# Two output projections: four Strassen units instead of three, with weight sums made by accumulating DMAs

## The chip, the core and the metric

The kernel runs on one core of a Trainium2 chip. A core has five engines that run independent instruction streams and meet only at semaphores: TensorE (PE in the profile; PEld is its weight load), VectorE (DVE), ScalarE (ACT), GpSimd (POOL) and SyncE (SP). Tensors sit in HBM, tiles in SBUF, and matmul results in banks of PSUM. DMAs move data between HBM and SBUF; SP issues most of them, GpSimd some, each from its own queue in the order of its program. The metric is the device time of one execution in microseconds (us).

## The reference, cut to what matters

Two layers on 512 tokens of width 1024, all in float32: an attention mixer, then an mLSTM mixer, each followed by a gated feed-forward block. The change touches only the second matrix of that block, `w_out`:

```python
D_FF = 2816
def swiglu(xn, w_in, w_out):
    gu = xn @ w_in
    return (jax.nn.silu(gu[..., :D_FF]) * gu[..., D_FF:]) @ w_out
...
h = h + swiglu(rms_norm(h, ffn_norm[i]), ffn_w_in[i], ffn_w_out[i])
```

So each layer multiplies a hidden matrix of 512 tokens by 2816 with weights of 2816 by 1024 and adds the result to the residual stream. After layer 1 a last norm follows.

## The kernel before

*Precision.* A float32 operand is split into a high part (rounded by a ScalarE copy, `split_chunk` L204 to L211 for weights, `split_operand` L1110 to L1116 for the hidden values) and a low part (VectorE: operand minus high part). Each product is made of three matmuls: high by high, high by low, low by high.

*Row tiles.* The 2816 rows of `w_out` are 22 tiles of 128, taken in pairs: 11 pairs `pi`. The hidden matrix is kept as `hid[pi]`, two row tiles by 512 tokens; `half(pi, t)` is one of its two halves of 256 tokens. The 1024 output columns form two halves n of 512.

*Units.* `output_products` (L1090) joins pair u with pair UNITS + u for u = 0, 1, 2. A unit is a 2 x 2 block product (two pairs by two column halves of weights, two pairs by two token halves of hidden values), and is computed as seven block products P1 to P7 (the Strassen-Winograd scheme) instead of eight. It needs sums of weight blocks and sums of hidden halves. The pairs left over, 6 to 10 (`REST`), are multiplied in the plain way, one item for each pair and column half.

*A product's weights.* `prepare_product` (L1121) loads the blocks that the product needs (512 KB each, SP's queue, tag `wraw` with three buffers; the block W11 goes to `tw`, tag `w8`, and stays there to become the running sum T; the second block of P5 in layer 0 goes to tag `t1`, one buffer). VectorE forms the sum, then `split_chunk` makes the high and low part (three buffers each), and the hidden operand is split. So the split of item n waits until TensorE has finished item n - 3. Layer 0 and layer 1 use two mirrored variants (`sums_of_rows` true and false): in layer 0 the matmuls of a product have 256 columns (tokens) and there are 24 of them, in layer 1 they have 512 columns (weights) and there are 12.

*Order.* `items` (L1211) lists the work: P1 of all units, P5 and P2 in turn, P6 and P7 with the first column half of the plain pairs between them, P3, then P4 with the second column half between, and a few plain items as a tail. `work` prepares an item two items (AHEAD) before its matmuls are issued; the first two are prepared while the input projection `ffn_in` still runs. `during` (L1189) runs in `ffn_in`'s blocks j and forms sums of hidden halves there, and in the last block it splits the operands of P1 and P2. The order of instructions on each engine is that of a scheduler which follows program order closely but moves ready work forward; within an engine the order is then fixed. After some products `then` (L1284, L1673) copies or adds banks of PSUM.

Of the kernel before, what the change touches and what calls it, by code (L numbers as in the profile page):

```python
# [11 lines left out]
F32 = mybir.dt.float32  # L12
F32R = mybir.dt.float32r
I32 = mybir.dt.int32
AF = mybir.ActivationFunctionType
ALU = mybir.AluOpType
# [55 lines left out]
def tile_hybrid_dilated_attn_mlstm(  # L72
# [124 lines left out]
    def load_chunk(src, shape, name):  # L197
        n = int(np.prod(shape[1:]))
        view = lambda t: t[:, :n].rearrange("p (a b) -> p a b", a=shape[1])
        raw = wp.tile([P, 1024], F32, tag="wraw", name=name + "_w", bufs=W_BUFS)  # L200
        nc.sync.dma_start(view(raw), src)
        return raw, n, view, name

    def split_chunk(chunk):  # L204

        raw, n, view, name = chunk
        hi = wp.tile([P, 1024], F32R, tag="whi", name=name + "_h", bufs=W_BUFS)
        lo = wp.tile([P, 1024], F32R, tag="wlo", name=name + "_l", bufs=W_BUFS)
        nc.scalar.activation(hi[:, :n], raw[:, :n], AF.Copy)
        nc.vector.tensor_tensor(lo[:, :n], raw[:, :n], hi[:, :n].bitcast(F32), op=ALU.subtract)  # L210
        return view(hi), view(lo)  # L211
# [878 lines left out]
    def output_products(layer, fp, wo, sums_of_rows, tail):  # L1090
# [3 lines left out]

        UNITS = 3
        REST = range(2 * UNITS, FC // 2)
        hid, ops, whl, sums, tw = [], {}, {}, [], []
        PARTS = ("P1", "P2", "P5", "P6", "P7", "P3", "P4")  # L1100
        ROWS = ({"P1": (0, 0), "P2": (1, 0), "P5": (0, 1), "P7": (1, 1), "P3": (1, 0), "P4": (1, 1)} if sums_of_rows else
                {"P1": (0, 0), "P2": (1, 0), "P5": (0, 1), "P6": (1, 1), "P7": (0, 0), "P3": (1, 1), "P4": (1, 0)})

        def half(pi, t):
            return hid[pi][:, :, t * HALF:(t + 1) * HALF]

        def subtract(out, x, y):
            nc.vector.tensor_tensor(out, x, y, op=ALU.subtract)

        def split_operand(name, u, src):  # L1110

            t = fp.tile([P, 2, 2, HALF], F32R, tag="op%d" % (UNITS * (PARTS.index(name) % 3) + u),
                        name="f%d%s_%d" % (layer, name, u))
            nc.scalar.activation(t[:, 0], src, AF.Copy)
            subtract(t[:, 1], src, t[:, 0].bitcast(F32))
            ops[name, u] = [[t[:, part, k] for k in range(2)] for part in range(2)]  # L1116

        def weight_rows(pi, n):
            return wo[pi * 2 * P:(pi + 1) * 2 * P, n * 512:(n + 1) * 512].rearrange("(k p) n -> p k n", p=P)

        def prepare_product(name, u):  # L1121
            nm = "f%d%s_%dw" % (layer, name, u)
            view = lambda t: t.rearrange("p (k n) -> p k n", k=2)

            def load(hk, n):
                return load_chunk(weight_rows(hk * UNITS + u, n), [P, 2, 512], nm)[0]
            if name == "P1":
                if u % 2 == 0:
                    tw.append(fp.tile([P, 2, 1024], F32, tag="w8", name="f%dT%d" % (layer, u), bufs=2))
                nc.sync.dma_start(view(tw[u // 2][:, u % 2]), weight_rows(u, 0))  # L1130
            t = tw[u // 2][:, u % 2]
            raw = load(*ROWS[name]) if name in ROWS and name != "P1" else t
            if sums_of_rows:

                if name == "P5":
                    a22 = fp.tile([P, 1024], F32, tag="t1", name=nm + "2")
                    nc.sync.dma_start(view(a22), weight_rows(UNITS + u, 1))
                    nc.vector.tensor_tensor(raw, raw, a22, op=ALU.add)
                elif name in ("P7", "P3"):
                    subtract(raw, raw, t)  # L1140
            else:

                if name in ("P5", "P6"):
                    subtract(t, raw, t)
                    raw = t
                elif name == "P7":
                    subtract(raw, t, raw)
                elif name == "P4":
                    subtract(raw, raw, t)
            whl[name, u] = split_chunk((raw, 1024, view, nm))  # L1150
            if sums_of_rows and name == "P5":
                subtract(t, raw, t)

            if name == "P5":
                split_operand(name, u, sums[u])
            elif name == "P6":
                split_operand(name, u, half(u, 1))
            elif name == "P7":
                subtract(sums[u], *((half(u, 1), half(u, 0)) if sums_of_rows else (half(UNITS + u, 1), half(u, 1))))
                split_operand(name, u, sums[u])  # L1160
            elif name == "P3":
                if not sums_of_rows:
                    subtract(half(u, 1), half(UNITS + u, 0), half(u, 1))
                split_operand(name, u, half(UNITS + u, 1) if sums_of_rows else half(u, 1))
            elif name == "P4":
                if sums_of_rows:
                    subtract(half(UNITS + u, 0), half(UNITS + u, 0), half(u, 1))
                split_operand(name, u, half(UNITS + u, 0 if sums_of_rows else 1))

        def prepare_rest(n, pi):  # L1170
            if pi not in ops:
                i = pi - REST[0]
                hi = fp.tile([P, 2, SEQ], F32R, tag="op%d" % (3 * UNITS + i), name="f%dhh%d" % (layer, pi))
                nc.scalar.activation(hi, hid[pi], AF.Copy)
                if i < 3:
                    tags = (("u2", 1), ("v5", 1)) if i == 0 else (("gu%d" % (2 - i), 1 + i),) * 2
                    lo = [fp.tile([P, SEQ], F32R, tag=tg, name="f%dhl%d" % (layer, pi), bufs=bufs)
                          for tg, bufs in tags]
                    for k in range(2):
                        subtract(lo[k], hid[pi][:, k], hi[:, k].bitcast(F32))  # L1180
                else:

                    t = xp.tile([P, 2, SEQ], F32R, tag="x%d" % (pi - 4), name="f%dhl%d" % (layer, pi))
                    subtract(t, hid[pi], hi.bitcast(F32))
                    lo = [t[:, k] for k in range(2)]
                ops[pi] = [hi[:, k] for k in range(2)], lo
            whl[n, pi] = split_chunk(load_chunk(weight_rows(pi, n), [P, 2, 512], "f%dw%d_%d" % (layer, n, pi)))

        def during(j, i):  # L1189
            u = (j - PLAIN) // 2 - (2 * UNITS - PLAIN // 2)  # L1190
            if i == 1 and 0 <= u < UNITS:
                sums.append(fp.tile([P, 2, HALF], F32, tag="sums", name="f%dS%d" % (layer, u), bufs=UNITS))
                if sums_of_rows:
                    subtract(sums[u], half(u, 1), half(u, 0))
                else:
                    nc.vector.tensor_tensor(sums[u], half(u, 1), half(UNITS + u, 1), op=ALU.add)
            if i == 4 and 0 <= u < UNITS:
                subtract(half(u, 1), *((half(UNITS + u, 1), sums[u]) if sums_of_rows else (sums[u], half(u, 0))))
            if j == FC - 2 and 3 <= i:
                for u in {3: (0,), 4: (1, 2)}.get(i, ()):  # L1200
                    split_operand("P1", u, half(u, 0))
                for u in {5: (0,), 6: (1, 2)}.get(i, ()):
                    split_operand("P2", u, half(UNITS + u, 0))

        PR = lambda name: [("product", name, u) for u in range(UNITS)]

# [1 line left out]
        rest = {n: [("rest", n, pi) for pi in REST] for n in range(2)}  # L1208
        last = rest[second][-tail:]
        merge = lambda *lists: [e for group in itertools.zip_longest(*lists) for e in group if e]  # L1210
        items = (PR("P1") + merge(PR("P5"), PR("P2")) + merge(PR("P6") + PR("P7"), rest[first]) + PR("P3")  # L1211
                 + merge(PR("P4"), rest[second][:-tail]) + last)

        def prepare(i):
# [22 lines left out]
    with ExitStack() as fctx:  # L1237
# [43 lines left out]
        def first_tiles():  # L1281
            for m in range(4):
                natural(m, F[0][m])
        last = work(product, plain, {("P1", 2): lambda: copy_half(0), ("P5", 2): lambda: copy_half(1),  # L1284
                                     ("P6", 2): lambda: add_sum(0), ("P7", 2): lambda: add_sum(1),
                                     ("P3", 2): first_tiles})
        for m in range(4):
            for b, w in last:
                tile_mm(F[1][m], m, b, w)
# [299 lines left out]
    with ExitStack() as fctx:  # L1589
# [79 lines left out]
        def plain(n, pi, a, w):  # L1669
            for t in range(2):  # L1670
                multiply_half(((c11, u_), (p5, c22))[n][t], a, t, w)

        last = work(product, plain, {("P1", 2): lambda: copy_banks(u_, c11), ("P5", 2): lambda: copy_banks(c22, p5),  # L1673
                                     ("P6", 2): lambda: add_banks((0, 1), u_), ("P7", 2): lambda: add_banks((2, 3), u_),
                                     ("P4", 0): lambda: outputs((0, 1), p5), ("P4", 1): lambda: outputs((2, 3), c22)})

        rest_of = bank("o", "last")
# [53 lines left out]
```

## Time and profile before

| what | value |
|---|---|
| three runs | 1412.66, 1413.14, 1413.24 us; median 1413.14 |
| profiled execution | 1413.13 us, span 1411.4 us, granted TensorE clock 0.998 |
| TensorE (PE) | 1400.3 us busy, 99% |
| VectorE (DVE) | 1044.6 us, 74% |
| ScalarE (ACT) | 633.8 us, 45% |
| GpSimd (POOL) | 118.5 us, 8% |
| layer 0's output projection (fo) | 732.0 to 846.9 us |
| layer 1's output projection (fin) | from 1292.5 us to the end |

How to read it: the span is the time between the first and the last instruction. A row of a timeline gives the start, the duration, engine, source line, operation, output tile <- input tiles, and in brackets how long the engine had been idle before and what ended that. Tiles of the projections carry names such as `f0P_1w_l` (layer 0, unit 1, low part of a product's weights), `f0T` (the running sum T), `f0P` (split hidden operands), `f0w_l` (weights of a plain item). The duration of a matmul contains its fill; matmuls overlap, so the distance from start to start is their cost. In the list of DMAs the last number is the time from issue to landing.

### The profile page before, as it was taken

Reading aid. Unit: us, or ns where it says so; the run is one execution under the profiler, and the core shown is the slowest. Engines: PE = TensorE matmul, PEld = TensorE weight load, DVE = VectorE, ACT = ScalarE, POOL = GpSimd, SP = SyncE. Lnnn points to the kernel's source line nnn. Section 1 sums busy time; section 2 is a strip of 40 time slices with the busy share of each in tenths; the row PEclk is TensorE's granted clock in tenths of the full one; section 3 lists DMA queues with packets and bytes.
Section 4 is the critical chain, followed back from the end, with each engine's and each line's share of the span. In section 5 each row is a group of like instructions: output and inputs, shape, how many; then the busy total and the mean of one; then the engine's idle time right before and its main releaser. Section 6 shows DMA issues by size and latency. Waiting matters only on the chain. (4 is left out here: it accounts for less than half of the span.)

```text
span 1411.4 us, 20838 instructions
## 1 busy us (share of the span) xinstructions
PE 1400.3 (99%) x8094; PEld 1236.4 (88%) x8094; DVE 1044.6 (74%) x1798; ACT 633.8 (45%) x1061; POOL 118.5 (8%) x193
## 2 busy tenths in 40 slices
PE   9999999999999999999999999999999999999998
PEld 7888888888888888999999988888888899999886
DVE  7866557566667298877887868898758888778884
ACT  5333224224225254445474343786534344457343
POOL 1011011002002000000000001113101230000001
PEclk9999999999999999999999999999999999999999
DMA  6346245335434444133234443224333553333442
GB/s 194 97 113 201 77 118 161 117 105 136 154 105 124 153 120 149 61 120 120 79 121 145 134 121 92 87 78 106 104 102 107 158 163 99 121 120 103 152 149 90
DMA packets 134650, 171.27 MB, mean 121 GB/s; under 512 B 8276, under 2 KB 110996, under 8 KB 134552
## 3 DMA queue, kind: packets, MB, share of 16 engines
q1 hardware_dynamic: 124848, 140.99, 32.2%
q0 software_dynamic: 8048, 27.84, 7.5%
q8 instruction: 63, 1.03, 0.3%
q10 hardware_dynamic: 1656, 1.12, 0.2%
q14 instruction: 35, 0.29, 0.1%
HBM read 154.19 MB, written 15.73 MB: 120 GB/s over the span
## 5 line engine op out<-in xcount | busy, mean ns | idle before, releaser
L240 PE MATMUL f0j<-n_h,f0j_h 128*128 128x512 f32 x96 | 37.5, 391 | 0.0
L240 PE MATMUL f1j<-n_h,f1j_h 128*128 128x512 f32 x96 | 37.5, 391 | 0.0
L240 PE MATMUL f1j<-n_h,f1j_l 128*128 128x512 f32 x96 | 37.4, 390 | 0.0
L240 PE MATMUL f0j<-n_h,f0j_l 128*128 128x512 f32 x96 | 37.4, 390 | 0.0
L240 PE MATMUL f1j<-n_l,f1j_h 128*128 128x512 f32 x96 | 37.4, 389 | 0.0
L240 PE MATMUL f0j<-n_l,f0j_h 128*128 128x512 f32 x96 | 37.4, 389 | 0.0
L1359 POOL MEMSET gates_h<- 128x1024 f32 x1 | 1.0, 959 | 380.5 <-PE fo L1251 380.5
L1251 PE MATMUL fo<-f0hh,f0w_h 128*128 128x512 f32 x80 | 31.2, 390 | 0.0
L1251 PE MATMUL fo<-f0hl,f0w_h 128*128 128x512 f32 x80 | 31.2, 390 | 0.0
L1251 PE MATMUL fo<-f0hh,f0w_l 128*128 128x512 f32 x80 | 31.1, 389 | 0.0
L539 DVE TENSOR_TENSOR rot<-rot,sinr 32x1024 f32<-32x1024 f32 x24 | 28.9, 1205 | 0.0
L1603 POOL DMA_DIRECT2D hD<-hB x32 | 20.6, 650 | 96.6 <-DVE hB L1600 96.0
L240 PE MATMUL mo<-n_h,mo_k_h 128*128 128x512 f32 x64 | 25.4, 396 | 0.0
L240 PE MATMUL mo<-n_h,mo_k_l 128*128 128x512 f32 x64 | 25.3, 395 | 0.0
L240 PE MATMUL mo<-n_l,mo_k_h 128*128 128x512 f32 x64 | 25.1, 393 | 0.0
L240 PE MATMUL mwo<-yo_l,mwo_k_h 128*128 128x512 f32 x64 | 25.1, 392 | 0.0
L240 PE MATMUL mqk<-n_h,mqk_k_h 128*128 128x512 f32 x64 | 25.1, 392 | 0.0
L240 PE MATMUL mqk<-n_l,mqk_k_h 128*128 128x512 f32 x64 | 25.1, 392 | 0.0
L240 PE MATMUL awo<-ao_h,awo_k_h 128*128 128x512 f32 x64 | 25.1, 392 | 0.0
L240 PE MATMUL mqk<-n_h,mqk_k_l 128*128 128x512 f32 x64 | 25.0, 391 | 0.0
L240 PE MATMUL mwo<-yo_h,mwo_k_l 128*128 128x512 f32 x64 | 25.0, 391 | 0.0
L240 PE MATMUL awo<-ao_h,awo_k_l 128*128 128x512 f32 x64 | 25.0, 390 | 0.0
(2249 smaller groups left out, 5354.8 us busy)
## 6 DMA issues: line engine op xcount, KB each, us to landing
f0j_w<-in_ffn_w_in_dram SPq DMA_DIRECT2D x28, 512.0 KB, 4.3
f1j_w<-in_ffn_w_in_dram SPq DMA_DIRECT2D x28, 512.0 KB, 4.0
f0w_w<-in_ffn_w_out_dram SPq DMA_DIRECT2D x10, 512.0 KB, 4.0
f1w_w<-in_ffn_w_out_dram SPq DMA_DIRECT2D x10, 512.0 KB, 4.2
awo_k_w<-in_attn_w_out_dram SPq DMA_DIRECT2D x8, 512.0 KB, 7.1
mv_k_w<-in_mlstm_w_in_dram SPq DMA_DIRECT2D x8, 512.0 KB, 3.7
mqk_k_w<-in_mlstm_w_in_dram SPq DMA_DIRECT2D x8, 512.0 KB, 3.7
mo_k_w<-in_mlstm_w_in_dram SPq DMA_DIRECT2D x8, 512.0 KB, 4.0
```

Source lines behind the costliest of these rows:

```text
L240: nc.tensor.matmul(acc, whl[a][:, k, m * P:(m + 1) * P], pairs[b][kk], start=(kk == 0 and (a, b) == SPLITS[0]), stop=(kk == nk - 1 and (a, ...
L539: nc.vector.tensor_tensor(sh, sh, sinr.unsqueeze(1).to_broadcast([R, 2, SEQ]), op=ALU.mult)
L1251: nc.tensor.matmul(acc, w[a_][:, k, m * P:(m + 1) * P], b[b_][k], start=(fresh and k == 0 and (a_, b_) == SPLITS[0]), stop=(k == 1 and (a_ ...
L1359: nc.gpsimd.memset(gh.bitcast(F32), 0.0)
L1603: nc.gpsimd.dma_start(hD[k // 4].rearrange("(b i) x -> i b x", i=R)[:, :, c0:c0 + R], t[R * a_:R * (a_ + 1)])
```

## The change

`UNITS` becomes 4: units join pairs u and 4 + u for u = 0 to 3, and three plain pairs (8, 9, 10) are left. The order of the items stays, except that P6 is no longer mixed with plain items. Most sums of weights are no longer made by VectorE from two loaded blocks: `add_rows` issues a DMA from GpSimd that adds a block of `w_out` in HBM onto a tile in SBUF, and `negate` flips a tile's sign on ScalarE where a difference is wanted. In layer 0, P5's second block is added this way onto the first, and T receives its last block after P7; in layer 1, T receives a block after P1, P5 and P7. VectorE keeps two sums per unit in layer 0 and one in layer 1. P5's weights of the odd units in layer 0 now go to tag `t1`. The operands of P2 are split when P2 is prepared instead of in the last block of the input projection, and `during` forms its sums in blocks j = 14 to 20 instead of 12 to 16. The high part of pair 10 moves to a tile of the `x` tags.

```diff
-        UNITS = 3
+        UNITS = 4
...
-        ROWS = ({"P1": (0, 0), "P2": (1, 0), "P5": (0, 1), "P7": (1, 1), "P3": (1, 0), "P4": (1, 1)} if sums_of_rows else
-                {"P1": (0, 0), "P2": (1, 0), "P5": (0, 1), "P6": (1, 1), "P7": (0, 0), "P3": (1, 1), "P4": (1, 0)})
+        ROWS = ({"P2": (1, 0), "P5": (0, 1), "P7": (1, 1), "P4": (1, 1)} if sums_of_rows else
+                {"P2": (1, 0), "P7": (0, 0), "P3": (1, 1)})
...
+            def add_rows(to, hk, n):
+
+                nc.gpsimd.dma_start(view(to), weight_rows(hk * UNITS + u, n), accum_op=ALU.add)
+
+            def negate(x):
+                nc.scalar.activation(x, x, AF.Copy, scale=-1.0)
...
-            raw = load(*ROWS[name]) if name in ROWS and name != "P1" else t
+            in_place = ("P1", "P6", "P3") if sums_of_rows else ("P1", "P5", "P6", "P4")
+            if sums_of_rows and name == "P5" and u % 2:
+                raw = fp.tile([P, 1024], F32, tag="t1", name=nm + "1")
+                nc.sync.dma_start(view(raw), weight_rows(u, 1))
+            else:
+                raw = t if name in in_place else load(*ROWS[name])
             if sums_of_rows:
                 if name == "P5":
-                    a22 = fp.tile([P, 1024], F32, tag="t1", name=nm + "2")
-                    nc.sync.dma_start(view(a22), weight_rows(UNITS + u, 1))
-                    nc.vector.tensor_tensor(raw, raw, a22, op=ALU.add)
-                elif name in ("P7", "P3"):
-                    subtract(raw, raw, t)
-            else:
-                if name in ("P5", "P6"):
-                    subtract(t, raw, t)
-                    raw = t
-                elif name == "P7":
-                    subtract(raw, t, raw)
-                elif name == "P4":
-                    subtract(raw, raw, t)
-            whl[name, u] = split_chunk((raw, 1024, view, nm))
-            if sums_of_rows and name == "P5":
-                subtract(t, raw, t)
+                    add_rows(raw, 1, 1)
+                elif name == "P7":
+                    nc.vector.tensor_tensor(raw, raw, t, op=ALU.add)
+                    add_rows(t, 1, 0)
+            elif name == "P7":
+                nc.vector.tensor_tensor(raw, raw, t, op=ALU.add)
+                add_rows(t, 1, 0)
+            whl[name, u] = split_chunk((raw, 1024, view, nm))
+            if sums_of_rows:
+                if name == "P5":
+                    subtract(t, raw, t)
+                elif name == "P6":
+                    negate(t)
+            elif name in ("P1", "P5"):
+                negate(t)
+                add_rows(t, int(name == "P5"), 1)
+            elif name == "P6":
+                negate(t)
 
-            if name == "P5":
+            if name == "P2":
+                split_operand(name, u, half(UNITS + u, 0))
+            elif name == "P5":
                 split_operand(name, u, sums[u])
...
-            u = (j - PLAIN) // 2 - (2 * UNITS - PLAIN // 2)
+            u = j // 2 - (FC // 2 - UNITS)
...
-                for u in {3: (0,), 4: (1, 2)}.get(i, ()):
-                    split_operand("P1", u, half(u, 0))
-                for u in {5: (0,), 6: (1, 2)}.get(i, ()):
-                    split_operand("P2", u, half(UNITS + u, 0))
+                split_operand("P1", i - 3, half(i - 3, 0))
...
-        items = (PR("P1") + merge(PR("P5"), PR("P2")) + merge(PR("P6") + PR("P7"), rest[first]) + PR("P3")
+        items = (PR("P1") + merge(PR("P5"), PR("P2")) + PR("P6") + merge(PR("P7"), rest[first]) + PR("P3")
                  + merge(PR("P4"), rest[second][:-tail]) + last)
```

More of the change, by code (lines that the diff above doesn't have):

```diff
@@ L1158, in prepare_product @@
             elif name == "P7":
-                subtract(sums[u], *((half(u, 1), half(u, 0)) if sums_of_rows else (half(UNITS + u, 1), half(u, 1))))
+                subtract(sums[u], half(u, 1), half(u, 0) if sums_of_rows else half(UNITS + u, 1))
                 split_operand(name, u, sums[u])
@@ L1172, in prepare_rest @@
                 i = pi - REST[0]
-                hi = fp.tile([P, 2, SEQ], F32R, tag="op%d" % (3 * UNITS + i), name="f%dhh%d" % (layer, pi))
+                hi = (fp.tile([P, 2, SEQ], F32R, tag="op%d" % (3 * UNITS + i), name="f%dhh%d" % (layer, pi)) if i < 2 else
+                      xp.tile([P, 2, SEQ], F32R, tag="x%d" % (pi - 4), name="f%dhh%d" % (layer, pi)))
                 nc.scalar.activation(hi, hid[pi], AF.Copy)
[L1175 to L1185, printed above, removed]
+                tags = (("u2", 1), ("v5", 1)) if i == 0 else (("gu%d" % (2 - i), 1 + i),) * 2
+                lo = [fp.tile([P, SEQ], F32R, tag=tg, name="f%dhl%d" % (layer, pi), bufs=bufs) for tg, bufs in tags]
+                for k in range(2):
+                    subtract(lo[k], hid[pi][:, k], hi[:, k].bitcast(F32))
                 ops[pi] = [hi[:, k] for k in range(2)], lo
@@ L1283, in first_tiles @@
                 natural(m, F[0][m])
-        last = work(product, plain, {("P1", 2): lambda: copy_half(0), ("P5", 2): lambda: copy_half(1),
-                                     ("P6", 2): lambda: add_sum(0), ("P7", 2): lambda: add_sum(1),
-                                     ("P3", 2): first_tiles})
+        last = work(product, plain, {("P1", 3): lambda: copy_half(0), ("P5", 3): lambda: copy_half(1),
+                                     ("P6", 3): lambda: add_sum(0), ("P7", 3): lambda: add_sum(1),
+                                     ("P3", 3): first_tiles})
         for m in range(4):
@@ L1671, in plain @@
                 multiply_half(((c11, u_), (p5, c22))[n][t], a, t, w)
-        last = work(product, plain, {("P1", 2): lambda: copy_banks(u_, c11), ("P5", 2): lambda: copy_banks(c22, p5),
-                                     ("P6", 2): lambda: add_banks((0, 1), u_), ("P7", 2): lambda: add_banks((2, 3), u_),
+        last = work(product, plain, {("P1", 3): lambda: copy_banks(u_, c11), ("P5", 3): lambda: copy_banks(c22, p5),
+                                     ("P6", 3): lambda: add_banks((0, 1), u_), ("P7", 3): lambda: add_banks((2, 3), u_),
                                      ("P4", 0): lambda: outputs((0, 1), p5), ("P4", 1): lambda: outputs((2, 3), c22)})
```

## The prediction

> **What bounds the kernel now.** I read the page first, then the waits of TensorE, the chain, and the two output projections.
>
> ```profile
> span 1411.4 us, 20838 instructions
> PE 1400.3 (99%) x8094; PEld 1236.4 (88%) x8094; DVE 1044.6 (74%) x1798; ACT 633.8 (45%) x1061; POOL 118.5 (8%) x193
> PE idle L108 <- DVE idle_w L103: 1.5, 1, 1.5
> PE m2num L1512 <- DVE m1yt L1533: 1.1, 1, 1.1
> ...
> 1131.36 2.87 PE f1j_c L1017 x24
> 1300.82 2.72 PE finp L1633 x12
> 1360.66 8.16 PE finp L1633 x36
> ...
> L1251 PE MATMUL fo<-f0P,f0P_0w_h x112: 277/283/284, 732.0 to 813.8; 128*128 128x256 f32 x112
> L1251 PE MATMUL fo<-f0hh,f0w_l x80: 388/389/390, 761.3 to 846.8; 128*128 128x512 f32 x80
> ```
>
> TensorE is busy for 99% of the span, and its longest waits (1.5 and 1.1 us) lie at the start and in the mLSTM, none in an output projection. So TensorE's own work sets the time. The chain gives the price of that work: 24 matmuls of 256 columns take 2.87 us (2.88 in most rows beside it, which I use), 12 of 512 columns take 2.72, 36 take 8.16. The first product of layer 0's projection starts at 732.0 and the last matmul at 846.8. Between them 21 products of 2.88 and ten plain items of 24 wide matmuls (2 x 2.72 = 5.44) come to 114.9: there is no gap to be won, only work to be removed, and none of it may be replaced by a wait.
>
> **TensorE's work (UNITS 3 to 4).** A unit replaces two row-tile pairs in two column halves, that is four plain items, 4 x 5.44 = 21.76 us, by seven products. In layer 0 a product is 24 matmuls of 256 columns: 7 x 2.88 = 20.16, so 1.60 us is saved. In layer 1 it is 12 of 512 columns: 7 x 2.72 = 19.04, so 2.72 is saved. Together 4.32 us, 0.31% of the span. That is all the change can give; everything below can only take from it. The smallest difference that a measurement of this kernel tells from none is about 0.2%, 2.8 us, so a new wait of 1.5 us already hides the gain.
>
> **VectorE and ScalarE.** The prices come from the rows around the first sums of layer 0.
>
> ```profile
> 734.80 1.22 DVE L1138 TENSOR_TENSOR f0P_0w_w<-f0P_0w_w,f0P_0w 128x1024 f32<-128x1024 f32 x1
> 735.93 0.69 DVE L1108 TENSOR_TENSOR f0P<-f0S,f0P 128x512 fp32r<-128x512 f32 x1
> 736.53 1.22 DVE L1108 TENSOR_TENSOR f0T<-f0P_0w_w,f0T 128x1024 f32<-128x1024 f32 x1
> 737.67 2.54 DVE L210 TENSOR_TENSOR f0P_0w_l<-f0P_0w_w,f0P_0w_h 128x1024 fp32r<-128x1024 f32 x2
> ...
> 730.68 1.99 ACT L1174 ACTIVATE f0hh<-f0hid 128x1024 fp32r<-128x1024 f32 x2
> 737.89 1.06 ACT L209 ACTIVATE f0P_0w_h<-f0P_0w_w 128x1024 fp32r<-128x1024 f32 x1 [0.73 <-PE fo L1251]
> ...
> 1287.76 0.61 ACT L1114 ACTIVATE f1P<-f1S 128x512 fp32r<-128x512 f32 x1
> 1288.28 1.04 ACT L1174 ACTIVATE f1hh<-f1hid 128x1024 fp32r<-128x1024 f32 x1
> 732.00:757.90 25.90, 25.90 (x218) 25.90 (x217) 22.37 (x24) 17.52 (x26) 0.00 (x0) 1.00 0.49 163
> ```
>
> From start to start, a 128x1024 operation of VectorE costs 1.13 us (1.14 below), a 128x512 one 0.60; ScalarE takes 0.97 for 128x1024 and 0.52 for 128x512. Layer 0 loses two of the four weight sums per unit on VectorE (P5's and P3's) and gets one negation on ScalarE; layer 1 loses three of four and gets three negations. The fourth unit adds seven operand splits and three short sums, the two plain pairs fewer take two 128x1024 splits from each of the two engines. The sums and differences of the hidden halves (L1190 to L1199) move to the last four blocks of the input projection; P2's operand splits (L1203) move out of its last two products into the output stage. Now sixteen products stand in a row before the first plain item, 46.1 us in layer 0. VectorE's share there is 16 x 1.14 for the low parts, 4 x 1.14 for the sums left, about 17 short ones at 0.60 and 2.5 more: 35.5 of 46.1, less than the 22.37 of 25.90 that the window shows today. In layer 1, ScalarE is the fuller one: from P1_0's copy to P2_3's 12 copies, 8 negations, 9 operand splits and 3.4 of others are 27.5 of 30 us. It fits, because a copy needs to come only two products ahead, but the cover is thin: each negation waits for VectorE's low part of the same weights. I followed it item by item with these prices: the closest is P5_1's low part, done at 1306.9 for a product at 1308.8. Cost 0.
>
> **The accumulating DMAs.** GpSimd issues 8 in layer 0 and 12 in layer 1, each 512 KB onto weights in SBUF. SP issues 26 loads instead of 31 in layer 0 and 22 instead of 31 in layer 1, so three more transfers in each layer. No accumulating DMA is in this trace. Nearest rows:
>
> ```profile
> DMA to landing us min/median/max: 4.5/4.5/4.5
> L1617 POOL DMA_DIRECT2D gbc<-in_final_norm_dram x1: 534/534/534, 1279.9 to 1279.9; - x1
> 1284.50 2.79 POOL L1618 TENSOR_SCALAR gbc<-gbc 128x1024 f32<-128x1024 f32 x1 [4.04 <-DMA gbc<-in_final_norm_dram]
> a0pT<-a0pD POOLq DMA_DIRECT2D x2, 960.0 KB, 8.1
> a3pT<-a3pD POOLq DMA_DIRECT2D x2, 960.0 KB, 9.0
> ...
> GB/s 5 10 0 0 13 190 369 381 329 9 10 0 0 0 0 108 214 228 243 195 227 90 0 0 0 13 258 86 287 284 289 268 238 221 3 158 348 139 1 224
> f0P_0w_w<-in_ffn_w_out_dram SPq DMA_DIRECT2D x3, 512.0 KB, 4.8
> f0P_1w_w<-in_ffn_w_out_dram SPq DMA_DIRECT2D x2, 512.0 KB, 4.3
> ```
>
> Lower end: a plain 512 KB load on the same queue, 4.5 us. Upper end: 960 KB on that queue, 9.0 us, since an accumulation must read what it adds to and so takes in 1024 KB. I take the lower row plus another 512 KB at the 381 GB/s of the busiest slice, 1.4 us: 5.9, nearer to gbc's row because only 512 KB is written. Both ends stay for the range; a gain below zero is excluded, as TensorE has no wait to lose.
>
> [...]
>
> **Layer 1's accumulations are hidden.** P1_0's low part starts at 1287.88, its negation ends at 1290.0, GpSimd has been free since 1284.50 + 2.79 (gbc stands ahead in its queue).
>
> ```profile
> 1287.88 1.23 DVE L210 TENSOR_TENSOR f1P_0w_l<-f1T,f1P_0w_h 128x1024 fp32r<-128x1024 f32 x1 [0.28 <-ACT f1P_0w_h L209]
> 1289.67 1.06 ACT L209 ACTIVATE f1P_1w_h<-f1T 128x1024 fp32r<-128x1024 f32 x1 [0.35 <-PE f1j_p L1017]
> ```
>
> P5_0 is the fifth item, at 1292.5 + 4 x 2.72 = 1303.4. Its copy can't start before P1_1's product has freed a weight buffer (1297.9), and 2.4 us of lead remain. So the DMA may take about 11 us. P5 to P6 and P7 to P4 have at least four items, 10.9 us. Cost 0 at 5.9 and at 9.0. Behind them in GpSimd's queue stand only the final products with gbc.
>
> **Layer 0's P5 is not hidden.** Here W12 is loaded first, then W22 is added by DMA, then it is split: two transfers in series, where today both loads run at once and VectorE adds. Today the third one already waits:
>
> ```profile
> 741.37 0.37 SPq L1137 DMA_DIRECT2D f0P_2w<-in_ffn_w_out_dram  x1
> 747.08 1.23 DVE L1138 TENSOR_TENSOR f0P_2w_w<-f0P_2w_w,f0P_2w 128x1024 f32<-128x1024 f32 x1 [1.11 <-DMA f0P_2w<-in_ffn_w_out_dram]
> 749.96 2.35 DVE L210 TENSOR_TENSOR f0P_2w_l<-f0P_2w_w,f0P_2w_h 128x1024 fp32r<-128x1024 f32 x2
> ```
>
> The load issued at 741.37 was waited for until 747.08; P5_2's low part was done at 751.1 for a product at 732.0 + 7 x 2.88 = 752.2. In the changed kernel the items run P1_0 to P1_3, then P5 and P2 in turn: P5_2 is item 8 (755.0), P2_2 item 9 (757.9), P5_3 item 10 (760.8). P5_3's weights go to tag t1, which P5_1 holds until its low part. P5_1's copy waits for product 3 to end (743.5; the row at 737.89 shows this wait today), ends at 744.6, its low part at 746.1. SP then issues W12 at 746.1; with the window's 4.8 us for such a load and 0.1 for GpSimd to wake it is 751.0, and with 5.9 the sum has landed at L = 756.9.
>
> VectorE's order decides who waits. Behind P5_3's sum (T minus the row, 1.14) stands P2_2's low part (1.14 to 1.22), needed at 757.9, its use being the third matmul. So L must be at most 755.7. P5_3's own low part comes after one operand split and one short sum, L + 4.7, needed at 761.0: L at most 756.3. P5_2 itself, loaded from 740.9, asks only for a DMA under 6.4 (740.9 + 4.8 + 0.1, then 1.14 + 0.60 + 1.22 of VectorE). The wait is then 756.9 - 755.7 = 1.2 us. At the ends, a load of 4.3 and a DMA of 4.5 give L = 755.0 and no wait; today's 5.7 for the load into t1 and 9.0 give 760.9 and 5.2. GpSimd has nothing behind these until P7. P7's accumulation feeds P3 seven items later: hidden.
>
> **Moves priced at nothing.** After layer 0, GpSimd clears gates_h last instead of first.
>
> ```profile
> 847.05 0.96 POOL L1359 MEMSET gates_h<- 128x1024 f32 x1 [380.47 <-PE fo L1251]
> 850.69 0.52 POOL L1380 MEMSET mneg<- 128x512 f32 x1
> L1368 PE MATMUL gates<-n_h,gates_h x8: 388/389/390, 858.9 to 862.0; 128*128 128x512 f32 x8
> ```
>
> That is some 4 us later, and its matmuls start at 858.9. In layer 1 P4's four products follow one another without plain items between, but their weight buffers still come free three items ahead.
>
> **Sum.** The profiled execution took 1413.13 us for a span of 1411.4, beside a median of 1413.14, so it stands for the runs. 1413.1 - 4.3 + 1.2 = 1410.0.
>
> **Rivals.** *A: no wait at all* (L at most 755.7, a DMA near gbc's 4.5): 1408.8. For it: same size, same queue. Against: gbc is not added to anything. *B: slow accumulation*, 8.1 to 9.0 as the 960 KB rows: wait 3.4 to 5.2, 1412.2 to 1414.0, no measurable change. For it: the bytes read. Against: those transfers also write 960 KB. *C: slower than before by one mechanism*: the addition runs far below the rate of a copy. Layer 0 gives back the whole gain at 9.0 us per DMA and is slower by 0.2% from 11.9; at 14 us the wait is 9.3, and layer 1's P5_0 waits 3 more: 1421. Against: nothing in the trace moves so slowly at 2 KB a row; for it: no row shows an addition. *D: the sums leave VectorE but ScalarE's negations become layer 1's limit*, so the change moves its load instead of removing it: 2 us lost there if each of the eight negations in P1 and P5 costs 0.25 us of waiting, 1412.0. Against: my item by item count.
>
> **How the numbers follow.** Forecast (wait 0.3 to 2.2) 0.37, A 0.22, B 0.22, C 0.12, D 0.07. The forecast's own range is 1409.1 to 1411.0. For 8 in 10 I go from 1408.4 (A with a little noise) to 1414.0 (the end of B), which leaves out C and little else. Faster by over 0.2% means below 1410.3, a wait under 1.5: A and four fifths of the forecast, 0.52. Slower means above 1416: C and a rest, 0.14. Within 0.2%: 0.34.
>
> **What would show it.** Right: a span of TensorE of 113.3 us plus the wait in layer 0's projection and 1.60 + 2.72 us less matmul time; a wait of TensorE for P2_2's or P5_3's low part near 758, with VectorE idle before the line of T minus P5_3, released by the accumulating DMA; no TensorE wait in layer 1. Wrong: a landing time of the additions outside 4.5 to 9.0; a wait in layer 1 behind a negation; matmuls of the fourth unit that take more than 0.120 or 0.227 us each; or a wait in the last blocks of the input projection, where the sums now crowd.

## The result and the profile after

The changed kernel takes 1415.41 us (median of 22 runs, 1413.65 to 1418.46), the kernel before 1412.88 (22 runs, 1412.09 to 1413.82). The ratio is 1.0019, 95% interval 1.0013 to 1.0026: a little slower, where 1410.0 was forecast. The profiled execution took 1414.34 us for a span of 1412.2.

The page's head after the change, then TensorE's waits (us in total, times, longest):

```profile
span 1412.2 us, 21010 instructions
PE 1396.3 (99%) x8154; PEld 1235.7 (88%) x8154; DVE 1045.6 (74%) x1810; ACT 658.9 (47%) x1093; POOL 142.8 (10%) x213
```

```profile
PE fo L1260 <- DVE f0P_2w_l L210: 4.2, 2, 3.4
PE idle L108 <- DVE idle_w L103: 1.5, 1, 1.5
PE m2num L1521 <- DVE m1yt L1542: 1.2, 1, 1.2
```

TensorE does 4.0 us less (1400.3 to 1396.3), close to the 4.3 counted. New waits of 4.2 us in all stand ahead of the others, both in layer 0. The name `f0P_2w_l` is shared by the products of unit 2, and their places in TensorE's timeline tell them apart (P5_2 is item 8, from 755, P2_2 item 9):

```profile
755.83 0.39 PE L1260 MATMUL fo<-f0P,f0P_2w_l 128*128 128x256 f32 x1 [0.72 <-DVE f0P_2w_l L210]
762.40 0.39 PE L1260 MATMUL fo<-f0P,f0P_2w_l 128*128 128x256 f32 x1 [3.44 <-DVE f0P_2w_l L210]
```

The first, of 0.7 us, is for P5_2's own low part, which the prediction had on time; the second, of 3.4, is for P2_2's, where the prediction put the wait. The two output projections as stretches of time, first before, then after (busy time of each engine, granted clock, DMA share, GB/s):

```profile
732.00:846.80 114.80, 114.80 (x745) 105.34 (x744) 85.15 (x99) 50.96 (x67) 0.00 (x0) 1.00 0.41 129
1292.50:1404.10 111.60, 111.60 (x511) 93.11 (x510) 81.51 (x107) 51.01 (x71) 4.51 (x4) 1.00 0.41 127
```

```profile
732.00:849.60 117.60, 113.44 (x815) 107.31 (x813) 88.88 (x106) 59.77 (x77) 7.12 (x6) 1.00 0.49 127
1295.60:1404.60 109.00, 109.00 (x499) 90.76 (x498) 80.13 (x111) 66.92 (x90) 17.70 (x15) 1.00 0.61 140
```

Layer 1 gained 111.6 - 109.0 = 2.6 us without a wait, as forecast (2.72). Layer 0's first matmul came at 731.7, so its stage took 117.9 us: 3.1 longer than before, not 1.6 shorter. The difference of the two profiled executions, 1.2 us, adds up from -0.3 (an earlier start), +3.1, +0.3 (between the layers), -2.6, +0.3 (after the last matmul) and +0.4 outside the span.

The chain of waits after the change shows where layer 0's time went (start, us, what):

```profile
745.72 7.26 DMA f0P_3w<-in_ffn_w_out_dram
752.97 0.02 issue
753.00 0.04 POOLq L1130
753.04 0.48 issue
753.52 0.01 POOLq L1130
753.53 6.43 DMA f0P_3w<-in_ffn_w_out_dram
759.97 0.02 issue
...
760.07 1.06 ACT f0P_3w_h L209
761.14 1.23 DVE f0P_2w_l L210
762.36 0.04 issue
762.40 12.71 PE fo L1260 x103
```

Load, then addition, then the split, with TensorE at the end of it. GpSimd's first issue and VectorE's queue beside it, from the timeline (start, us, what, and in brackets the idle time before and who ended it):

```profile
744.79 1.18 POOL L1130 DMA_DIRECT2D f0P_2w_w<-in_ffn_w_out_dram  x1 [20.59 <-DVE f0P L1108]
...
752.82 1.23 DVE L1108 TENSOR_TENSOR f0T<-f0P_2w_w,f0T 128x1024 f32<-128x1024 f32 x1 [4.19 <-DMA f0P_2w_w<-in_ffn_w_out_dram]
759.99 1.23 DVE L1108 TENSOR_TENSOR f0T<-f0P_3w,f0T 128x1024 f32<-128x1024 f32 x1 [3.01 <-DMA f0P_3w<-in_ffn_w_out_dram]
761.13 1.22 DVE L210 TENSOR_TENSOR f0P_2w_l<-f0P_2w_w,f0P_2w_h 128x1024 fp32r<-128x1024 f32 x1
```

VectorE stood idle twice for an addition: P5_2's, issued at 744.79, was there after 8.0 us, P5_3's at 759.97. P2_2's low part (at 761.13), which needs neither, stood behind the second. P5_2's low part came late too, behind the first.

### The profile page after: what moved, and what is told of

It reads as the page before. It is cut to its first block, busy times and chain, and to the rows that moved or that the text cites. A ratio compares the mean times of both kernels' runs of the same rounds, so it can differ in the third digit from the quotient of the medians.

```text
span 1412.2 us, 21010 instructions
## 1 busy us (share of the span) xinstructions
PE 1396.3 (99%) x8154; PEld 1235.7 (88%) x8154; DVE 1045.6 (74%) x1810; ACT 658.9 (47%) x1093; POOL 142.8 (10%) x213
## 3 DMA queue, kind: packets, MB, share of 16 engines
q0 software_dynamic: 13488, 38.33, 12.2%
## 4 chain that ended last, share of the span: by engine, by line
PE 91%; DVE 5%; ACT 2%; DMA 1%; issue 1%; ACTq 0%; POOLq 0%; DVEq 0%
PE fo L1260 7%; PE f1j_u L1017 5%; PE f0j_u L1017 5%; PE f0j L240 5%; PE f1j L240 5%; PE f1j_p L1017 3%; PE f0j_p L1017 3%; PE f1j_c L1017 3%; PE f0j_c L1017 3%; PE mwo L240 3%; PE awo L240 3%; PE mo L240 3%; PE finu L1642 2%; PE finc L1642 2%; PE finp L1642 2%; PE a3g12v L298 2%
## 5 line engine op out<-in xcount | busy, mean ns | idle before, releaser
L240 PE MATMUL awo<-ao_l,awo_k_h 128*128 128x512 f32 x64 | 24.9, 390 | 0.0
L240 PE MATMUL mwo<-yo_h,mwo_k_h 128*128 128x512 f32 x64 | 24.9, 391 | 0.0
L240 PEld LDWEIGHTS f1j<-n_h,f1j_l 128*128 128x128 f32 x96 | 18.0, 188 | 3.8
```

Of the source, the lines that this page charges most:

```text
L240: nc.tensor.matmul(acc, whl[a][:, k, m * P:(m + 1) * P], pairs[b][kk], start=(kk == 0 and (a, b) == SPLITS[0]), stop=(kk == nk - 1 and (a, ...
```

## The experiments

Theory S: the loss is the wait for layer 0's P5, made of a load and an accumulating DMA in series. Rival C: an accumulation is slow in itself. Rival D: layer 1 loses something too. Rival E: something other than the wait (time outside the span, the granted clock) costs as much. All medians below are to be held against 1412.8 to 1413.0 for the kernel before.

**The changed kernel again.**

> The changed kernel once more, for its scatter. Theory S (the wait for the fifth product's weights in layer 0, two transfers in series, sets the loss): TensorE waits 3 to 6 us for P2_2's and P5_3's weights in layer 0's output projection and nowhere else new; time 1414 to 1416. Rival E (something outside the span or a lower granted clock costs as much as the wait): the wait is the same 4 us in a slow and in a quick execution, and the granted clock or the time outside the span differs.

Measured: 1416.02 us (1414.04 to 1417.51, 11 runs), ratio 1.0021 (1.0012 to 1.003). TensorE's wait was 3.8 us in the profiled execution, so less than the 4.2 of the first, yet it took 1415.24 us and layer 0's stage 118.9. The stretches around the wait show why, and some rows of TensorE's timeline:

```profile
757.00:762.00 5.00, 1.95 (x17) 1.75 (x16) 2.48 (x3) 1.06 (x1) 0.00 (x0) 1.00 0.65 173
762.00:766.00 4.00, 4.00 (x23) 4.00 (x24) 4.00 (x7) 2.14 (x4) 0.00 (x0) 0.64 0.43 131
766.00:770.00 4.00, 4.00 (x33) 4.00 (x32) 2.41 (x4) 3.22 (x6) 0.00 (x0) 0.93 0.43 112
```

```profile
761.94 0.39 PE L1260 MATMUL fo<-f0P,f0P_2w_l 128*128 128x256 f32 x1 [3.05 <-DVE f0P_2w_l L210]
762.52 0.40 PE L1260 MATMUL fo<-f0P,f0P_2w_h 128*128 128x256 f32 x2
762.88 0.42 PE L1260 MATMUL fo<-f0P,f0P_2w_h 128*128 128x256 f32 x2
...
763.95 0.63 PE L1260 MATMUL fo<-f0P,f0P_2w_h 128*128 128x256 f32 x2
764.59 0.63 PE L1260 MATMUL fo<-f0P,f0P_2w_h 128*128 128x256 f32 x2
```

Some 1.2 us after the stall of 3.05 the granted clock drops: three matmuls take 0.64 us instead of 0.36. At 0.64 and 0.93 of the clock over four microseconds each, 4 x 0.36 + 4 x 0.07 = 1.7 us are lost. In the first profiled execution the clock stayed at 1.00 here, although its stall was longer, 3.44 us:

```profile
762.00:766.00 4.00, 3.60 (x30) 3.60 (x31) 4.00 (x7) 2.42 (x4) 0.00 (x0) 1.00 0.47 130
```

So the waits are those of S, and E holds in part, in a form that I had not thought of: a lower clock behind the stall, in one profiled execution and not in the other, worth 1.7 us and so less than the wait itself.

**P5_3 in a tile of its own.** Its load and addition stand beside P5_1's in the program, and no longer wait for P5_1's low part (at 746.21 in the trace): they are issued at 733.48 and 737.86.

```diff
-            if sums_of_rows and name == "P5" and u % 2:
-                raw = fp.tile([P, 1024], F32, tag="t1", name=nm + "1")
-                nc.sync.dma_start(view(raw), weight_rows(u, 1))
...
+        def p5_rows(u):
...
+            if u % 2:
+                raw = fp.tile([P, 1024], F32, tag="t1" if u == 1 else "op13", name=nm + "1")
+                nc.sync.dma_start(view(raw), weight_rows(u, 1))
+            else:
+                raw = load_chunk(weight_rows(u, 1), [P, 2, 512], nm)[0]
+            nc.gpsimd.dma_start(view(raw), weight_rows(UNITS + u, 1), accum_op=ALU.add)
+            return raw
...
+            if sums_of_rows and name == "P5":
+                raw = early.pop(u) if u in early else p5_rows(u)
+                if u == 1:
+                    early[3] = p5_rows(3)
```

> Only P5_3's rows get a tile of their own, loaded and added to together with P5_1's, so P5_3's load no longer waits for P5_1's low part to free the buffer; P5_2 stays as it is. Theory S: the 3.4 us for P2_2's low part and most of the rest go, 0 to 1 us is left for P5_2's addition: 1411 to 1412. If contention of the transfers and not the order is what counts, P5_2 lands 8 us or more after its issue as now, and 2 to 4 us of wait stay: 1413 to 1415.

Measured: 1410.32 us (1409.58 to 1411.63, 11 runs), ratio 0.9982 (0.9973 to 0.9991). No wait is left in layer 0's projection; its stage, 733.4 to 847.0, takes 113.6 us (113.3 by TensorE's work). P5_2's addition landed 5.9 us after its issue, against 8.0 in the changed kernel; P5_3's load no longer runs beside it. One buffer, and what it made wait, was enough to turn the change from a gain into a loss: S. The kernel is still 1.7 us above the 1408.6 that 1412.9 less TensorE's 4.3 would give, with no wait in the projection to account for it.

**P5 with two loads, as before.** VectorE adds, and the first block of every unit is loaded into the buffers of tag `wraw` again; the rest is the changed kernel.

```diff
...
-                if name == "P5":
-                    add_rows(raw, 1, 1)
+                if name == "P5":
+                    a22 = fp.tile([P, 1024], F32, tag="t1", name=nm + "2")
+                    nc.sync.dma_start(view(a22), weight_rows(UNITS + u, 1))
+                    nc.vector.tensor_tensor(raw, raw, a22, op=ALU.add)
```

> Layer 0's P5 is made as before (both blocks loaded at once, VectorE adds), all else as in the changed kernel: four units, three transfers fewer onto GpSimd's queue at this place. Theory S: the wait goes but for about 1 us (four additions of 1.13 us come back on VectorE, about 40 of 46 us busy over the sixteen products): 1411 to 1412. Rival E: 1414 or more.

Measured: 1409.48 us (1408.24 to 1411.03, 9 runs), ratio 0.9977 (0.9967 to 0.9987). What remains in layer 0 is a wait for ScalarE's copies of the sums between P5 and P6:

```profile
PE fo L1258 <- ACT fo L1281: 0.8, 1, 0.8
```

It came out 1.5 us below the expectation, which had taken off the wait alone. The changed kernel, timed beside these two (1416.02), is 5.7 us above the tile of its own and 6.5 above the two loads, while its profiled execution waited 3.8: more than the wait goes with it. How much of that is the clock is not shown.

**P5_2 and P5_3 later in the order, their transfers earlier** (p5_rows as above, with t1 for every odd unit).

```diff
-        items = (PR("P1") + merge(PR("P5"), PR("P2")) + PR("P6") + merge(PR("P7"), rest[first]) + PR("P3")
+        p5s = PR("P5")
+        middle = p5s[:2] + PR("P2") + p5s[2:] if sums_of_rows else merge(p5s, PR("P2"))
+        items = (PR("P1") + middle + PR("P6") + merge(PR("P7"), rest[first]) + PR("P3")
...
+                if name == "P2" and u == 1:
+                    early.update({v: p5_rows(v) for v in (2, 3)})
```

> Layer 0's items in the order P1, P5_0, P5_1, P2_0 to P2_3, P5_2, P5_3, and the load and the accumulating DMA of P5_2 and P5_3 are issued together with P2_1's weights, several products ahead. Theory S: the wait of 4.2 us goes, nothing else changes: 1415.4 - 4.2 = 1411.2, down to 1409.5 if unprofiled executions wait longer than the profiled one. Rival E: 1414 or more, although TensorE no longer waits in layer 0. Rival C (an accumulation is slow by itself): its landing time stays over 6 us, and the time falls only because it is hidden.

Measured: 1413.95 us (1413.52 to 1414.62, 11 runs), ratio 1.0007 (0.9998 to 1.0016), not the 1411.2 expected. Of P2_2's wait 2.6 us stayed, with 0.9 in two others of this projection; behind it stand rows of the timeline:

```profile
PE fo L1274 <- DVE f0P_2w_l L210: 2.6, 1, 2.6
```

```profile
745.47 1.18 POOL L1131 DMA_DIRECT2D f0P_2w_w<-in_ffn_w_out_dram  x1 [21.76 <-DVE f0P_0w_l L210]
748.24 1.19 POOL L1131 DMA_DIRECT2D f0P_3w<-in_ffn_w_out_dram  x1 [1.59 <-DVE f0P_1w_l L210]
754.29 1.22 DVE L1108 TENSOR_TENSOR f0T<-f0P_2w_w,f0T 128x1024 f32<-128x1024 f32 x1 [6.11 <-DMA f0P_2w_w<-in_ffn_w_out_dram]
757.76 1.23 DVE L1108 TENSOR_TENSOR f0T<-f0P_3w,f0T 128x1024 f32<-128x1024 f32 x1 [0.50 <-DMA f0P_3w<-in_ffn_w_out_dram]
```

The edit brought P5_3's addition forward (748.24 against 753.53), but P5_2's not at all (745.47 against 744.79). Issued 2.8 us apart, the two ran beside each other and landed after 8.8 and 9.5 us, and T minus P5_2 still stood ahead of P2_2's low part on VectorE. In this run the earlier place in the program did not help, since the additions did not run alone and an urgent split was queued behind their consumer. TensorE's work and 3.5 us of waits would give 1412.1; I have no cause for the other 1.8. The granted clock was 1.00 around the wait, and E, which asked for no wait at all, is not tested here.

**Plain DMAs in place of the additions.**

```diff
-                nc.gpsimd.dma_start(view(to), weight_rows(hk * UNITS + u, n), accum_op=ALU.add)
+                kind = {} if sums_of_rows and name == "P5" else {"accum_op": ALU.add}
+                nc.gpsimd.dma_start(view(to), weight_rows(hk * UNITS + u, n), **kind)
```

> In layer 0's P5 the accumulating DMAs from GpSimd become plain ones of the same size from the same queue, at the same places in the order; P5's weights are then the second block alone, so the first is loaded and written over. Theory S1 (two transfers in series in a stretch where the queues are full; the addition is hardly slower than a copy): the second transfer still lands 5 to 6 us after its issue and 2 to 4 us of wait stay: 1412.5 to 1415. Rival S2 (the addition itself costs 2 us or more over a copy there): it lands in 4 to 4.5 us, P5_3's load beside it in about 5, and 0 to 1 us of wait is left: 1410 to 1411.5.

Measured: 1411.01 us (1410.23 to 1411.9, 11 runs), ratio 0.9987 (0.9978 to 0.9996). Its chain, its wait, and the landing times of the tile that P5_2's transfer fills (the longest of the three is that transfer's):

```profile
745.17 6.03 DMA f0P_3w<-in_ffn_w_out_dram
...
751.77 4.13 DMA f0P_3w<-in_ffn_w_out_dram
```

```profile
PE fo L1261 <- DVE f0P_2w_l L210: 0.9, 1, 0.9
```

```profile
L1131 POOL DMA_DIRECT2D f0P_2w_w<-in_ffn_w_out_dram x1: 704/704/704, 744.3 to 744.3; - x1
DMA to landing us min/median/max: 3.8/5.0/6.2
```

At the same places in the order a copy lands in 6.2 and 4.1 us where the additions took 8.0 and 6.4, and P5_3's load beside it takes 6.03 instead of 7.26. GpSimd's issue takes 0.70 us instead of 1.18. The two earlier places show the same sign: 7.3 against 10.0 for P5_1, 5.6 against 6.2 for P5_0. So both are at work: two transfers in series leave 0.9 us of wait even when they are copies, and the addition adds 1.8 to 2.3 us over a copy where it counts (0.6 to 2.7 over the four) and slows its neighbour by 1.2. Time and wait fit S2; the landing times are mixed, since P5_2's copy took 6.2 us and not S2's 4 to 4.5.

**One layer at a time.** Each keeps the functions of before, with three units, for the other layer.

```diff
-        hid, during, prepare, work = output_products(0, fp, ffn_w_out[0], True, 2)
+        hid, during, prepare, work = output_products_three(0, fp, ffn_w_out[0], True, 2)
```

> The change in layer 1 alone, layer 0 as before. Theory S: layer 1 gains its 2.7 us in full and nothing waits there: 1412.9 - 2.7 = 1410.2 (up to 1410.6 if the 0.4 us outside the span belong to it). Rival D (the negations on ScalarE or GpSimd's accumulations cost layer 1 something): 1411 to 1413.

> The change in layer 0 alone, layer 1 as before. Theory S: 1412.9 - 1.6 for the matmuls + 4.2 of wait + about 1 to 2 for the clock = 1416.5 to 1418, slower than the full change by layer 1's 2.7. Rival D: about 1413 to 1415.

Measured: layer 1 alone 1410.84 us (1410.09 to 1411.91, 11 runs), ratio 0.9986 (0.9977 to 0.9994); layer 0 alone 1417.34 (1415.89 to 1418.77, 5 runs), ratio 1.0033 (1.002 to 1.0045). The two differences, -1.9 and +4.6, add up to +2.6; the whole change gave +2.5 and +3.1 in its two sets of runs. The median of layer 1 alone lies between S's 1410.6 and D's 1411, but its trace has no wait of TensorE in that projection, and the stage takes 109.1 us, its gain but for 0.2. So D, a loss in that projection, falls; where the rest of the 2.7 stays, the run does not show.

**Without accumulating DMAs.** Four units, every sum on VectorE; the cut shows layer 0's part.

```diff
...
-                if name == "P5":
-                    add_rows(raw, 1, 1)
-                elif name == "P7":
-                    nc.vector.tensor_tensor(raw, raw, t, op=ALU.add)
-                    add_rows(t, 1, 0)
+                if name == "P5":
+                    a22 = fp.tile([P, 1024], F32, tag="t1", name=nm + "2")
+                    nc.sync.dma_start(view(a22), weight_rows(UNITS + u, 1))
+                    nc.vector.tensor_tensor(raw, raw, a22, op=ALU.add)
+                elif name in ("P7", "P3"):
+                    subtract(raw, raw, t)
...
```

> Four units, but every sum of weights on VectorE as before, with no accumulating DMA and no negation: what the fourth unit gives without the DMAs. TensorE's work is the changed kernel's (4.3 us less than before). By the prices of the prediction VectorE has 44.6 us of work in the first sixteen products of layer 0, which take TensorE 46.1, so almost no slack: if that holds, waits of 0 to 2 us and 1409 to 1411; if the order of its queue makes TensorE wait, 2 to 6 us and 1411 to 1415.

Measured: 1412.45 us (1411.98 to 1413.65, 11 runs), ratio 0.9998 (0.9989 to 1.0006). Layer 0's projection runs from 732.1 to 845.2 without a wait, 113.1 us, the full gain; layer 1's takes 112.2, more than before. VectorE in the first products of both, and the waits:

```profile
732.00:778.00 46.00, 46.00 (x386) 46.00 (x385) 40.09 (x45) 25.85 (x35) 0.00 (x0) 1.00 0.43 138
1292.00:1335.00 43.00, 42.41 (x187) 34.72 (x186) 38.26 (x42) 24.73 (x30) 0.00 (x0) 1.00 0.47 147
```

```profile
PE finu L1628 <- ACT f1P_3w_h L209: 0.9, 1, 0.9
PE finu L1628 <- DVE f1P_1w_l L210: 0.6, 1, 0.6
```

The accumulating DMAs pay in layer 1, where a product is shorter (2.72 us) and three of four sums are replaced; in layer 0 VectorE had room for the sums. Of layer 1's 3.2 us, these rows name 1.5; the rest I did not trace.

**Vector sums in layer 0, accumulating DMAs in layer 1.** The edit of the last run, in layer 0 alone.

> Four units in both layers; layer 0's sums of weights all on VectorE (as in the run without accumulating DMAs, where layer 0's projection took 113.1 us with no wait), layer 1's by accumulating DMAs (as in the changed kernel, 109.0 us with no wait). If the two stages stand alone, both gains are kept in full: 1412.9 - 1.7 - 2.6 = 1408.6, granted clock 0.998 to 0.999 and a spread of under 2 us. If the stages disturb each other (the second layer's accumulations reach back into the first, or the order of VectorE's queue changes), a wait of 1 us or more shows in one of them: 1409.6 or more.

Measured: 1410.29 us (1409.39 to 1411.34, 11 runs), ratio 0.9981 (0.9972 to 0.999). The stages take 113.2 and 109.0 us, both gains in full. The profiled execution, 3.4 us below the one before, starts layer 0's stage 0.8 us earlier, but 0.8 us more pass between the layers and 0.8 more after the last matmul, which I can't put down to a part. The intervals of this kernel, of the two loads (0.9977) and of the own tile (0.9982) overlap: all three beat the kernel before by about 0.2%, and none is shown to be the best.

**A stall without accumulating DMAs.** To see whether the clock falls because of the stall, the kernel with two loads makes P2_2's low part several times over: six times in a first run, as here, and three times in a second.

```diff
-        nc.vector.tensor_tensor(lo[:, :n], raw[:, :n], hi[:, :n].bitcast(F32), op=ALU.subtract)
+        for _ in range(6 if name == "f0P2_2w" else 1):
+            nc.vector.tensor_tensor(lo[:, :n], raw[:, :n], hi[:, :n].bitcast(F32), op=ALU.subtract)
```

> The kernel whose layer-0 P5 uses two loads (1409.5), with P2_2's low part made six times over on VectorE instead of once: no accumulating DMA is near, but TensorE must wait about 3.2 us for it and some 1.4 us for the product behind, as in the changed kernel. Theory G (a stall of TensorE of about 3 us lets the granted clock fall for some us in part of the executions, whatever causes the stall): 1409.5 + 4.6 + about 1 = 1415, executions spread over 3 us with granted clocks down to 0.996. Rival (the scatter comes from the accumulating DMAs): 1409.5 + 4.6 = 1414.1, spread of 1 to 2 us, clock 0.998 to 0.999.

> P2_2's low part made three times instead of six, so three VectorE operations of 1.14 us fewer ahead of TensorE: the stall falls from 8.3 to about 4.9 us. Theory G (a stall near 3 to 5 us lets the clock fall in part of the executions): 1409.5 + 4.1 (4.9 less the 0.8 us that this kernel waits anyway) = 1413.6 where the clock stays, 1.5 to 2 us more where it falls; a mixture, median 1413.6 to 1415.5, clocks of 0.996 to 0.999. If the clock did not depend on the stall: 1413.6, spread under 2 us, clock 0.999 throughout.

Measured: six times, 1419.11 us (1418.09 to 1419.98, 5 runs), ratio 1.0044 (1.0031 to 1.0057); three times, 1411.96 (1411.22 to 1414.56, 11 runs), ratio 0.9996 (0.9987 to 1.0005). The stalls missed their aim, since other operations were put between the repeats: 8.3 and 2.1 us instead of 4.6 and 4.9. The wait and two stretches of the first, then the wait of the second:

```profile
PE fo L1259 <- DVE f0P_2w_l L211: 8.3, 1, 8.3
```

```profile
762.00:766.00 4.00, 0.00 (x0) 0.00 (x0) 4.00 (x5) 0.00 (x0) 0.00 (x0) 0.57 0.69 190
766.00:770.00 4.00, 3.52 (x18) 3.52 (x19) 3.44 (x6) 0.53 (x1) 0.00 (x0) 0.57 0.58 202
```

```profile
PE fo L1259 <- DVE f0P_2w_l L211: 2.1, 1, 2.1
```

With 8.3 us the clock is already down when TensorE resumes (0.57), and all five executions have a mean granted clock of 0.995 to 0.997. With 2.1 us it is 0.998 or 0.999 in nine of eleven, and the two others are the slowest (1414.02 and 1414.56). The changed kernel, stalled 3.0 to 3.4 us after a first 0.7 or 0.8, has 0.997 or less in 20 of its 33 executions, the kernel before, timed beside it, in none of 31. GpSimd issued nothing in layer 0's projection before 769 us in these two kernels, so a stall of 8.3 us is enough by itself to bring the clock down. That the 3 us of the changed kernel are enough too is carried over from this, not shown. At 8.3 us the kernel is 9.6 slower than with two loads, for 7.5 us more of wait.

## Why the prediction was wrong

Two steps failed. The wait in layer 0 was put at 1.2 us and is 4.2: the sum of two landing times behind it was too small. With the measured wait the sum gives 1413.1 - 4.3 + 4.2 = 1413.0, still within the range of 1408.4 to 1414.0. What carried the median to 1415.41 is a second step: everything beside matmuls and that wait was put at nothing, and 2.4 us lie there, only in part explained.

- **TensorE's work: right.** 4.0 us less busy time; layer 1's stage fell by 2.6 of 2.72, and layer 0's takes 113.1 to 113.6 in the versions without a wait, 113.3 by the prediction's count.
- **Layer 1's accumulations hidden: right.** They land in 6.0 to 9.8 us, within the 11 that P5_0 leaves, and no wait appears.

```profile
L1130 POOL DMA_DIRECT2D f1T<-in_ffn_w_out_dram x12: 1194/1203/1261, 1293.6 to 1355.2; - x12
DMA to landing us min/median/max: 6.0/6.6/9.8
```

- **The ends for an addition, 4.5 to 9.0 us: too narrow.** The 9.8 here and the 10.0 of P5_1 in layer 0 lie outside, which the prediction named as a sign of being wrong. TensorE waited for neither; the additions that it did wait behind took 8.0 and 6.4.
- **VectorE and ScalarE at cost 0: right** as far as TensorE shows no wait for them; ScalarE's negations (D) cost nothing that shows.
- **The wait for P5 in layer 0: the right place, the wrong size.** SP issued P5_3's load at 745.72 (746.1 forecast). Then the load took 7.26 us, not the 4.8 of today's row; the wake of GpSimd 0.56, not 0.1; the addition 6.43, not 5.9. L became 759.97 instead of 756.9, and by the prediction's own rule 759.97 - 755.7 = 4.3 us of wait; 4.2 came, 0.7 of it already at P5_2, whose addition took 8.0 where 6.4 was allowed. The failing step is the sum of two landing times taken from rows in which such a transfer has fewer neighbours. The largest part, 2.5 us, is the load: it ran beside P5_2's addition (issued at 744.79, landed after 8.0) and other weights, and the plain copies show 1.2 of it to be the addition's doing. The loads of 4.3 and 5.7 at the two ends came from rows without an addition beside them.
- **What an addition costs over a copy.** The runs have 0.6 to 2.7 us between addition and copy at the same places; my 1.4, an estimate for another 512 KB at the 381 GB/s of the busiest slice before the change, lies among them, and falls short of the 1.8 and 2.3 of P5_2 and P5_3. That an addition takes in 1024 KB was my inference and was not shown: the page counts 512 KB for each (queue q0 has 27.84 MB before and 38.33 with the twenty), and no more than for a plain copy (38.33 too with four of the twenty made copies). No addition in the changed kernel's projections came near the 4.5 us of `gbc`'s load, on which rival A stood (6.0 at best).
- **Put at nothing: what lies beside the matmuls and the wait.** The first profiled execution has 1.3 us more than the 1413.0, in pieces of 0.5 us or less (0.4 of it outside the span), at a clock of 1.00 behind the stall; the median is another 1.1 above it. In the second profile 1.7 us of such an excess is the granted clock. Not all of it hangs on the stall: the tile of its own and the vector sums in layer 0 have no wait in either projection, and yet take 1410.3, 1.7 above the 1408.6 of the count (the first waits 1.1 us for `a0pT` long before, in its profiled execution; the second does not). So a part comes with the stall and a part with the change itself; the cause of the second part stays open, and the runs do not divide the two.
- **The rivals.** A (no wait, 1408.8) was not the changed kernel. The two versions that lose P2_2's wait took 1410.32 and 1409.48, the second with 0.8 us of another wait. B had the right size of wait (3.4 to 5.2), but by a slower addition, not by the load, and the time lies above its 1414.0. C asked for additions of 11.9 us or more and had 6.0 to 10.0. D's loss in layer 1 did not show.

## What to carry to other kernels

An accumulating DMA onto a tile that must be loaded first is two latencies in a row (here 7.26 and 6.43 us), and here it slowed the transfer beside it (7.26 us, against 6.03 beside a plain copy): use it where its result is due several items later, and keep a vector addition of two parallel loads where the lead is short. Look at what stands behind the consumer in its engine's queue, since that, and not the consumer itself, may be what the matmuls wait for. When TensorE runs near 100%, a new stall can cost more than its length: here 7.5 us more of wait cost 9.6, and 1.7 us went to a lower clock behind a stall of 3.05 in one profiled execution, nothing behind one of 3.44 in another.

## What the runs showed of the hardware

- After a stall of 3.05 us TensorE's granted clock went down for some 3 us: three matmuls took 0.64 us instead of 0.36, and the clock was 0.64 and 0.93 over the two stretches of 4 us behind the stall. After one of 3.44 in another execution of the same kernel it stayed at 1.00. With a stall of 8.3 us it was 0.57 in the profiled execution, and all five executions have a mean of 0.995 to 0.997. From what length of a stall on the clock falls, the runs do not show.
- An accumulating DMA of 512 KB takes GpSimd 1.18 us to issue, a plain one 0.70 in the same place. Two of them issued 2.8 us apart landed after 8.8 and 9.5 us, against a median of 6.6 in layer 1.
- The time outside the span is 1.8 us in the kernel before, 2.15 in the changed one and 1.8 again with P5_2 and P5_3 reordered, which has as many accumulating DMAs. So their number does not decide it, and I have no cause for it.
